# A hybrid pool / mLSTM block on one core: summed weight operands kept in DRAM for the second token half, and another order at the passage to the mLSTM outputs

## The chip, the cores and the metric

One Trainium2 chip; the kernel runs on one of its cores. The metric is the device time of one execution in microseconds (us). It was timed three times before the change: 2134.82, 2144.59 and 2145.74 us, median 2144.59. One more execution was taken by the hardware profiler.

## The reference, cut to what matters

The block takes 2048 tokens of width 1024 and a context of 256 tokens. Both are normalised and modulated, and projected by one matrix `w_in`; the projections feed a pooling mixer and a bidirectional mLSTM whose start state comes from the context. Then follow an output projection, a second norm and a SwiGLU layer. All in float32.

```
hx = modulate(rmsnorm(x, norm1[l]), sh1, sc1)
px, qx, kx, vx, ox, gx = project(hx, w_in[l], ...)     # pool, q, k, v, o, gates
_, st_f, st_b = mlstm_bidir(qc, kc, vc, gc, zero, zero)  # context: states alone
hx_m, _, _ = mlstm_bidir(qx, kx, vx, gx, st_f, st_b)
...
c_new = decay * c0 + einsum('bhs,bhsv,bhsd->bhvd', wk, vc, kc)
h     = num / maximum(abs(den), exp(-m))
...
mix_x = concatenate([pool_x, mlstm_output(hx_m, ox)]) @ w_out[l]
x = x + g1 * mix_x
x = x + g2 * swiglu(modulate(rmsnorm(x, norm2[l])), w_up[l], w_down[l])
```

## The kernel before, in words

**Seven products instead of eight.** A projection onto 2 x 128 output columns is done for one half of the tokens (1024 of 2048) at a time. The weight block of 1024 x 256 is cut into four blocks A11, A12, A21, A22 of 512 x 128, the tokens likewise, and the eight block products are replaced by seven, for which four of the seven weight operands are sums of blocks: s1 = A21 + A22 (operand 3), s2 = s1 - A11 (4), A11 - A21 (5) and A12 - s2 (2). `operands` (L586) makes them: `wsum` (L591) adds on VectorE (L593), `split` (L145) then makes a high part by a cast on ScalarE (L147) and a low part by a subtraction on VectorE (L150). Operands 0 and 1 go to tiles `vt`, the others to `wh` and `wl`, of which there are five buffers each. `unit` (L625) does the seven products, `product` (L614) is one of them: 12 matmuls (L619 to L621). `ORDER` (L263) is the order of the operands, 0, 1, 4, 3, 5, 2, 6.

**The projection stage.** The first token half runs two units for q and k (`conv_unit`, convolution and silu behind them), two for o (`o_unit`, a sigmoid), two for the pooling (`pool_units`), through `run_units` (L670); the second half runs pooling, then q and k. `load_raws` (L658) loads the two weight columns of a unit, 512 KB each, on SP's queue into tiles `raw` (three buffers). The token blocks of a half (`Btile`) are loaded by `load_B` (L551), three of them as they are and four through tiles `hst` with a split. Beside all this run the modulation vectors (`ada_acc`, L525), whose weight rows `adaw` come by SP and are summed on VectorE.

**The last two units with the chunk sums.** The second half's two o units (L896 to L900) are done product by product in turn. Between their products, `chunk_step` (L981) is called: for each of the 2 context and 16 token chunks it loads kT and v (`dma_kv`, L867), transposes kT on TensorE, weights it on VectorE (`delta_a`, L913), multiplies it with v into a PSUM tile `pd` (`delta_b`, L924), and copies the result to the state tiles, the forward half and the backward half each for two pairs of heads: three copies on ScalarE (L938), the one of the backward half's second pair on VectorE (L936). `scan_step` (L940) then adds to state k + 1 the decayed state k, with four vector instructions (L943). The first eight scan steps run inside `chunk_step`, the last seven (L1012) behind the last chunk. `load_wo` (L947) prepares the output matrix in between.

**The mLSTM outputs.** 16 steps, chunk 7 down to 0 and then 15 down to 8 (`order`, L1165). `ml_a` (L1038) loads a chunk's operands, multiplies q and k into the PSUM tile `pqk`, takes eight exponentials on ScalarE (L1064) and multiplies both on VectorE (L1066). `ml_b` (L1069) makes the outputs in the four-bank PSUM tile `po`: L1081 from the chunk itself, L1087 from the two states, which are the forward state of the chunk and the backward one. `prep` (L1106) and `proj` (L1130) do gating, output projection and residual, `second_norm` the second norm. The chunks' work is shifted against each other: `ml_a` one chunk ahead, `prep` one behind `ml_b`, `proj` two.

**What sets the order.** The program is written in the order of the text; a planner then decides for each engine in which order its instructions stand in that engine's queue, from readiness in its own model and the order of the text, and `issue_after` forbids it to put an instruction ahead of a named one on the same engine. Each queue is worked off in order. PSUM has eight banks; a pool that is opened takes the place of closed ones and waits for their last readers. Before the change the output stage's pools lie one behind the other from the first bank: three banks `pm`, four `po`, one `pq`; the last two to be freed, those of `pd`, come under the end of `po` and under `pq`.

## Time and profile before

| what | us |
|---|---|
| timed executions | 2134.82, 2144.59, 2145.74 |
| their median | 2144.59 |
| the profiled execution | 2133.75 |
| its span, first to last instruction | 2132.0 |
| TensorE busy | 2022.3 (95%) |
| VectorE busy | 1411.3 (66%) |
| ScalarE busy | 903.2 (42%) |
| moved by DMA | 397.80 MB, mean 187 GB/s |

The profile shows one execution. PE is TensorE's matmuls, PEld its weight loads, DVE VectorE, ACT ScalarE, POOL GpSimd, SP the queue that issues most DMAs. L619 is line 619 of the kernel. `out<-in` names tiles; where buffers of different tiles share a place, the name is that of one of them (`h` is any token block or state tile). Waits show what an engine was idle for; windows give the busy time of each engine in a stretch, the clock granted to TensorE as a share of full speed, the share of the 16 DMA engines' time and what they moved.

### The profile page before, as it was taken

How to read it: one execution, taken by the hardware profiler on the slowest of the kernel's cores; microseconds unless marked ns; L12 is line 12 of the kernel's file. 1: busy time of each engine (PE TensorE's matmuls, PEld its weight loads, DVE VectorE, ACT ScalarE, POOL GpSimd, SP SyncE). 2: the span in 40 equal slices, each digit the busy share in tenths (PEclk: the TensorE clock that was granted, in tenths of full speed). 3: DMA queues.
4: the chain of work that ended last, by engine and by line, in shares of the span. 5: the costliest groups of instructions: out<-in, count | busy, mean ns of one | idle time of the engine just before them, and what ended most of it. 6: DMA issues, size and time to landing. Idle time of an engine off the chain costs nothing.

```text
span 2132.0 us, 27467 instructions
## 1 busy us (share of the span) xinstructions
PE 2022.3 (95%) x9482; PEld 1641.3 (77%) x9482; DVE 1411.3 (66%) x2398; ACT 903.2 (42%) x1792; POOL 231.5 (11%) x222
## 2 busy tenths in 40 slices
PE   7989999995899998999999999999999999999998
PEld 3988776674687776788888877888888788888887
DVE  6866889877365656766676578776777554447664
ACT  5644644455344544433333344333333344433442
POOL 1000123210333320000000000000000002004121
PEclk9999999996899999999999999999999999999999
DMA  8597666568477775434343267556655584644642
GB/s 278 162 291 230 204 229 197 161 184 231 136 219 238 213 220 176 148 97 147 100 141 112 96 199 249 187 188 203 188 186 194 177 325 141 221 148 157 229 162 99
DMA packets 355059, 397.80 MB, mean 187 GB/s; under 512 B 22388, under 2 KB 243160, under 8 KB 354152
## 3 DMA queue, kind: packets, MB, share of 16 engines
q1 hardware_dynamic: 308976, 324.62, 47.5%
q10 hardware_dynamic: 45944, 71.43, 10.3%
q8 instruction: 74, 1.21, 0.2%
q14 instruction: 65, 0.53, 0.1%
HBM read 269.44 MB, written 126.54 MB: 186 GB/s over the span
## 4 chain that ended last, share of the span: by engine, by line
PE 73%; DMA 11%; DVE 8%; issue 3%; ACT 3%; SPq 1%; POOL 1%; ACTq 0%; DVEq 0%; POOLq 0%
PE pa L619 8%; PE pa L620 8%; PE pa L621 8%; PE pdn L1356 7%; PE pdn L1358 7%; PE pdn L1357 7%; PE pg L619 4%; PE pg L621 4%; PE pg L620 4%; PE pb L619 2%; PE pb L621 2%; PE pb L620 2%; DMA hst<-s_hb 2%; PE pm L1138 2%; PE pm L1140 1%
## 5 line engine op out<-in xcount | busy, mean ns | idle before, releaser
L619 PE MATMUL pa<-h,wh 128*128 128x512 f32 x680 | 271.5, 400 | 8.1 <-ACT p L633 4.6
L621 PE MATMUL pa<-h,wl 128*128 128x512 f32 x680 | 270.6, 399 | 0.0
L620 PE MATMUL pa<-h,wh 128*128 128x512 f32 x680 | 270.4, 398 | 0.0
L147 ACT CAST wh<-ws 128x512 fp32r<-128x512 f32 x224 | 138.3, 620 | 299.1 <-PE pg L620 160.7
L1356 PE MATMUL pdn<-ow,op 128*128 128x512 f32 x616 | 236.8, 389 | 1.0 <-ACT op L147 1.0
L1357 PE MATMUL pdn<-ow,op 128*128 128x512 f32 x616 | 237.5, 389 | 0.0
L1358 PE MATMUL pdn<-ow,op 128*128 128x512 f32 x616 | 237.5, 389 | 0.0
L150 DVE TENSOR_TENSOR op<-ra,op 128x512 fp32r<-128x512 f32 x154 | 121.3, 794 | 156.3 <-ACT op L147 156.1
L150 DVE TENSOR_TENSOR wl<-ws,wh 128x512 fp32r<-128x512 f32 x224 | 156.7, 702 | 56.9 <-ACT wh L147 56.6
L147 ACT CAST op<-ra 128x512 fp32r<-128x512 f32 x154 | 95.2, 621 | 222.5 <-PE pdn L1358 220.0
L620 PE MATMUL pg<-h,wh 128*128 128x512 f32 x448 | 177.9, 397 | 2.4 <-DVE h L150 2.4
L619 PE MATMUL pg<-h,wh 128*128 128x512 f32 x448 | 177.5, 397 | 1.4 <-ACT h L147 1.4
L621 PE MATMUL pg<-h,wl 128*128 128x512 f32 x448 | 177.5, 396 | 1.1 <-DVE wl L150 1.1
L619 PEld LDWEIGHTS pa<-h,wh 128*128 128x128 f32 x680 | 128.9, 190 | 43.4 <-ACT p L633 6.4
L621 PEld LDWEIGHTS pa<-h,wl 128*128 128x128 f32 x680 | 128.9, 190 | 31.0 <-issue 1.2
L620 PEld LDWEIGHTS pa<-h,wh 128*128 128x128 f32 x680 | 128.9, 190 | 29.9 <-issue 0.5
L593 DVE TENSOR_TENSOR ws<-raw 128x512 f32<-128x512 f32 x110 | 78.8, 717 | 99.0 <-DMA raw<-in_w_up_dram 91.7
L1388 POOL TENSOR_TENSOR hr<-hr,o 128x1024 f32<-128x1024 f32 x8 | 21.8, 2740 | 1099.5 <-ACT o L1401 929.8
L1356 PEld LDWEIGHTS pdn<-ow,op 128*128 128x128 f32 x616 | 115.5, 188 | 25.2 <-ACT op L147 1.4
L1358 PEld LDWEIGHTS pdn<-ow,op 128*128 128x128 f32 x616 | 115.6, 188 | 24.2
L1357 PEld LDWEIGHTS pdn<-ow,op 128*128 128x128 f32 x616 | 115.6, 188 | 23.9
L1138 PE MATMUL pm<-h,mh 128*128 128x512 f32 x256 | 107.2, 419 | 7.1 <-ACT mh L147 3.7
(361 smaller groups left out, 4318.6 us busy)
## 6 DMA issues: line engine op xcount, KB each, us to landing
raw<-in_w_up_dram SPq DMA_DIRECT2D x88, 512.0 KB
ra<-s_act SPq DMA_DIRECT2D x66, 512.0 KB
s_act<-adaw SPq DMA_DIRECT2D x84, 256.0 KB
rwt<-s_t SPq DMA_DIRECT2D x77, 256.0 KB
adaw<-in_w_ada_dram SPq DMA_DIRECT2D x64, 256.0 KB
s_act<-g SPq DMA_DIRECT2D x63, 256.0 KB
raw<-in_w_in_dram SPq DMA_DIRECT2D x25, 512.0 KB
s_hb<-hb SPq DMA_DIRECT2D x7, 1792.0 KB
```

The source lines that it names most:

```text
L147: nc.scalar.copy(hi, src)
L150: eng_lo.tensor_tensor(lo, src, r32(hi), op=ALU.subtract)
L593: nc.vector.tensor_tensor(t, a, b, op=op)
L619: nc.tensor.matmul(ps, lhsT=ah[:, k], rhs=B[:, 0, k], start=st, stop=False, **kw)
L620: nc.tensor.matmul(ps, lhsT=ah[:, k], rhs=B[:, 1, k], start=False, stop=False, **kw)
L621: mm_last[0] = nc.tensor.matmul(ps, lhsT=al[:, k], rhs=B[:, 0, k], start=False, stop=(k == 3), **kw)
L1138: nc.tensor.matmul(pt, lhsT=mh[:, k], rhs=w[:, 0, k % 4], start=(k == 0), stop=False)
L1140: nc.tensor.matmul(pt, lhsT=mlo[:, k], rhs=w[:, 0, k % 4], start=False, stop=(k == 7))
L1356: nc.tensor.matmul(ps, lhsT=A[:, 0, ts_], rhs=W[:, 0], start=start, stop=False)
L1357: nc.tensor.matmul(ps, lhsT=A[:, 0, ts_], rhs=W[:, 1], start=False, stop=False)
L1358: nc.tensor.matmul(ps, lhsT=A[:, 1, ts_], rhs=W[:, 0], start=False, stop=stop)
L1388: nc.gpsimd.tensor_tensor(rows[u], rows[u], O[u][:, :, c_], op=ALU.add)
```

## The change

1. A DRAM tensor `s_w` for 6 weight blocks x 4 sums x 2 parts is added. In the first token half `operands` writes the high and low part of each of the four summed operands to it, by SP's queue, after having made them. In the second half it loads these eight tiles instead of making the sums and splits; of the second weight column only the upper half (A22) is then loaded. The weight block's number goes through the units' tuples.
2. In `delta_b` all four copies are done by ScalarE.
3. The last seven scan steps go from behind the last chunk into the loop of the outputs, one behind each of the first seven `ml_b`.
4. The PSUM pools of the output stage: of the three banks `pm`, one lies at the left and two at the right end, so that `po` and `pq` lie on banks that the units and transposes used, and two `pm` banks on those of `pd`. They are used in turn as before.
5. The exponentials of the first `ml_a` wait (in ScalarE's queue) for the last sigmoid alone, and no longer for the last copy of `delta_b`. The gate `copies[-4]` in `prep` now names another copy, since there are more of them.

```diff
     s_g = dram.tile([4, D], F32, name="s_g")
+    s_w = dram.tile([6, 4, 2, P, 512], F32, name="s_w")
...
-    def operands(raws, wp, early=2):
...
+    def operands(raws, wp, early=2, keep_=None, kept=None):
+        SUMS = (4, 3, 5, 2)
+        if kept is not None:
+            def fetch(i):
+                if i in SUMS:
+                    ops = [wp[0].tile([P, 4, P], F32R, name=n, bufs=5) for n in ("wh", "wl")]
+                    for e, t in enumerate(ops):
+                        with tc.issue_after(raw_last[0].ins):
+                            nc.sync.dma_start(r32(t.rearrange("p k c -> p (k c)")), kept[SUMS.index(i), e])
+                    return tuple(ops)
+                src = raws[0][:, 4 * i:4 * i + 4] if i < 2 else raws[1]
+                if i < early:
+                    hi, lo = (vtp.tile([P, 4, P], F32R, name="vt") for _ in range(2))
+                else:
+                    hi = wp[0].tile([P, 4, P], F32R, name="wh", bufs=5)
+                    lo = wp[0].tile([P, 4, P], F32R, name="wl", bufs=5)
+                split(src, hi, lo, nc.scalar, nc.vector)
+                return hi, lo
+            return fetch
...
             split(src, hi, lo, nc.scalar, nc.vector)
+            if keep_ is not None and i in SUMS:
+                for e, t in enumerate((hi, lo)):
+                    nc.sync.dma_start(keep_[SUMS.index(i), e], r32(t.rearrange("p k c -> p (k c)")))
...
-    def load_raws(srcs, other=None):
+    def load_raws(srcs, other=None, kept=False):
...
                 st = rwp.tile([P, KD, P], F32, name="raw")
+            if kept and raws:
+                st, src = st[:, 0:4], src[4 * P:]
...
-        for n, (srcs, sink, after) in enumerate(units):
-            make = operands(load_raws(srcs), [wp])
+        for n, (srcs, sink, after, w, half) in enumerate(units):
+            if half:
+                make = operands(load_raws(srcs, kept=True), [wp], kept=s_w[w])
+            else:
+                make = operands(load_raws(srcs), [wp], keep_=s_w[w])
...
                 nc.sync.dma_start(rows[:, t0:t0 + n], y[:, :n])
-        return in_cols(O_Q + i0 * P), sink, after
+        return in_cols(O_Q + i0 * P), sink, after, i0 // 2, half
...
                 pool_mm(*todo.pop(0))
-        return lambda half: [(in_cols(0), sink_of(0, half), after),
-                             (in_cols(256), sink_of(2, half), flush if half else after)]
+        return lambda half: [(in_cols(0), sink_of(0, half), after, 2, half),
+                             (in_cols(256), sink_of(2, half), flush if half else after, 3, half)]
...
             nc.scalar.dma_start(s_so[i * P:(i + 1) * P, b * 512:(b + 1) * 512], so)
-        return in_cols(O_O + i0 * P), sink, lambda: None
+        return in_cols(O_O + i0 * P), sink, lambda: None, 4 + i0 // 2, half
...
     uns = [o_unit(tmps[u], 1, 2 * u) for u in range(2)]
-    makes = [operands(load_raws(u[0], o), [wp], early=0) for u, o in zip(uns, (None, rxp))]
+    makes = [operands(load_raws(u[0], o, True), [wp], early=0, kept=s_w[u[3]]) for u, o in zip(uns, (None, rxp))]
...
                     o = dsts[d][:, 2 * p_:2 * p_ + 2, :].rearrange("p h v -> p (h v)")
-                    if d and p_:
-                        nc.vector.tensor_copy(o, pd[64:128, 0:258])
-                    else:
-                        copies.append(nc.scalar.copy(o, pd[d * 64:d * 64 + 64, 0:258]))
+                    copies.append(nc.scalar.copy(o, pd[d * 64:d * 64 + 64, 0:258]))
...
         chunk_step()
-    for i in range(NCH // 2, NCH - 1):
-        scan_step(i)
...
     pms = ExitStack()
-    pmp = pms.enter_context(psum("pm", 3))
+    pma = pms.enter_context(psum("pma", 1))
+    pmb = pms.enter_context(tc.tile_pool(name="pmb", bufs=2, space=PSUM, side="right", reuse_waits="tile"))
...
     pqp = p2s.enter_context(psum("pq", 1))
+    n_pm = [0]
+    class Banks:
+        def tile(self, shape, dt, name):
+            n_pm[0] += 1
+            return (pma if n_pm[0] % 3 == 0 else pmb).tile(shape, dt, name=name)
+    pmp = Banks()
...
         nc.gpsimd.tensor_tensor(wb, wb, qd, op=ALU.mult)
-        with tc.issue_after(last_act[0].ins), tc.issue_after(copies[-1 if n == 0 else -1].ins):
+        with tc.issue_after(last_act[0].ins), tc.issue_after((copies[-1] if n else last_act[0]).ins):
...
             H_[t] = ml_b(t, order[t], A_.pop(t))
+        if t < NCH // 2 - 1:
+            scan_step(NCH // 2 + t)
```

## Rows read from the trace of the kernel before

**Rows 1.** Page, part 1: busy us (share of the span) and instructions.
```profile
PE 2022.3 (95%) x9482; PEld 1641.3 (77%) x9482; DVE 1411.3 (66%) x2398; ACT 903.2 (42%) x1792; POOL 231.5 (11%) x222
```

**Rows 2.** Windows by stage: length, busy us per engine (instructions), clock, DMA share, GB/s.
```profile
186.00:318.00 132.00, 124.36 (x516) 96.67 (x515) 113.72 (x196) 77.14 (x124) 16.35 (x43) 0.97 0.68 219
318.00:418.00 100.00, 89.94 (x343) 65.66 (x342) 92.67 (x139) 43.11 (x71) 31.11 (x27) 0.97 0.58 186
418.00:477.00 59.00, 54.96 (x267) 44.71 (x265) 47.20 (x72) 31.85 (x59) 8.35 (x5) 0.97 0.57 176
477.00:517.00 40.00, 24.20 (x104) 19.43 (x104) 28.66 (x58) 17.32 (x43) 2.54 (x2) 0.68 0.78 211
517.00:545.00 28.00, 15.92 (x89) 12.92 (x89) 17.41 (x47) 14.44 (x47) 6.50 (x4) 0.67 0.74 213
545.00:830.00 285.00, 266.92 (x1458) 218.59 (x1456) 156.28 (x310) 123.70 (x378) 88.68 (x69) 0.97 0.65 199
```

**Rows 3.** TensorE's waits, 318 to 418: awaited, us in total, times, longest.
```profile
PE tp L750 <- DVE pd L782: 4.1, 4, 1.6
PE pb L619 <- DVE pre L713: 3.3, 1, 3.3
PE pg L620 <- DVE h L150: 1.2, 1, 1.2
PE tp L750 <- ACT pd L751: 0.8, 1, 0.8
```

**Rows 4.** TensorE's waits, 477 to 545.
```profile
PE pqk L1057 <- DVE raw L1066: 11.1, 3, 6.8
PE pd L930 <- ACT h L938: 6.5, 5, 4.4
PE pb L917 <- DMA kT<-s_k: 5.6, 1, 5.6
...
PE pqk L1057 <- DVE h L936: 1.4, 1, 1.4
```

**Rows 5.** Full stretch (columns as rows 2); SP's stores (ns min/median/max); DMA sizes.
```profile
296.00:326.00 30.00, 30.00 (x116) 22.96 (x117) 26.09 (x39) 13.21 (x23) 10.15 (x7) 0.94 1.01 362
...
L1236 SPq DMA_DIRECT2D s_act<-adaw x84: 319/320/1752, 878.1 to 1672.8; - x84
...
hst<-s_ha ACTq DMA_DIRECT2D x28, 256.0 KB
...
h<-s_hc SPq DMA_DIRECT2D x6, 1024.0 KB
```

**Rows 6.** VectorE's groups, 318 to 418: busy us, mean ns, idle before.
```profile
L150 DVE TENSOR_TENSOR wl<-ws,wh 128x512 fp32r<-128x512 f32 x13 | 9.9, 758 | 0.0
...
L593 DVE TENSOR_TENSOR ws<-ws,raw 128x512 f32<-128x512 f32 x4 | 2.7, 683 | 0.0
```

**Rows 7.** Timelines, 513 to 545, of TensorE, VectorE, ScalarE: start us, us, instructions [idle].
```profile
513.14 3.38 PE L930 MATMUL pd<-vt,kw 128*128 128x129 f32 x12 [0.84 <-ACT h L938]
...
524.02 2.59 PE L1081 MATMUL po<-vt,raw 128*128 128x129 f32 x16
...
540.74 2.76 PE L1081 MATMUL po<-vt,raw 128*128 128x129 f32 x16
...
517.85 1.67 DVE L943 SCALAR_TENSOR_TENSOR h<-h,decx 128x129 f32<-128x129 f32 x6
...
537.59 1.22 DVE L1066 TENSOR_TENSOR raw<-raw,pqk 128x1024 f32<-128x1024 f32 x1 [4.25 <-DMA kT<-s_k]
...
518.24 4.20 ACT L1064 ACTIVATE raw<-raw,tokq 128x128 f32<-128x128 f32 x14
```

**Rows 8.** The copies out of PSUM: VectorE's group, 477 to 517; ScalarE's line.
```profile
L936 DVE COPY h<-pd 64x258 f32<-64x258 f32 x10 | 4.3, 430 | 0.4
...
L938 ACT COPY h<-pd x45: 354/368/372, 437.1 to 516.6; 64x258 f32<-64x258 f32 x45
```

**Rows 9.** TensorE's longest wait, 186 to 318.
```profile
PE pa L619 <- ACT p L633: 3.8, 2, 3.3
```

## The prediction

> **What bounds the kernel now.** I read first the busy times: TensorE is busy for 95% of the 2132.0 us span [rows 1], so a gain can only come from the stretches in which it is not. The second view, busy time by stage, finds them [rows 2]. The reader should compare each length with TensorE's own time: the projection stage's first token half (186 to 318) leaves 132.0 - 124.4 = 7.6 us idle, its second half (318 to 418) 10.1, the last two units with the chunk sums beside them (418 to 477) 4.0. The passage (477 to 545) leaves 15.8 + 12.1 = 27.9 us in 68, at a granted clock of 0.68 and 0.67, a mixture of the two levels 1.2 and 2.4 GHz; the stages around it stand at 0.97. The mLSTM output stage (545 to 830) is 94% busy. The third view says what ended the idle times. In the second half it was VectorE or work queued on it: four waits make 9.4 of the 10.1 us [rows 3], and VectorE is busy 92.7 of those 100 us [rows 2]. In the passage it was a chain: VectorE's product of weights and scores 11.1 us, ScalarE's copy out of PSUM 6.5, one kT transfer 5.6, VectorE's copy 1.4 [rows 4].
>
> **The change part by part.** The sum is made against the profiled execution, 2133.75 us, that is the span of 2132.0 and 1.75 around it. The three timed executions have a median of 2144.59, which is 10.84 above; the profiled one stands at their quick end (2134.82). The sum is a difference, so I add it to the median.
>
> *A, stores in the first half.* Six units each write 8 operands (4 sums, high and low part) of 128 x 512 x 4 bytes = 256 KB: 48 stores, 12.6 MB. Issuing one takes SP 0.32 us, as the equal store of the MLP shows [rows 5], 15 us in 132; behind each on SP wait the weight loads of the next unit, the ada rows and the convolution's outputs. The operand buffer is freed only after its store; there are five of each, a unit uses five, so the next user comes a unit (some 20 us) later. The load on the DMA engines is the real price: 12.6 MB over 132 us is 95 GB/s on top of 219, at a share of 0.68 [rows 2]; in proportion the share becomes 0.68 x 314/219 = 0.97. From 296 to 326, where the token blocks of the second half come in, the engines are already full (1.01 at 362 GB/s [rows 5]). About one unit's stores and the first unit's kept operands fall there: 2.1 + 2.1 - 0.3 (the half weight load that is saved) = 3.9 MB, 10.9 us at 362 GB/s. Bounds: 0, if all of it hides behind the prefetch, and 11. A gain is excluded, since nothing is taken from this half. I take 4: the stalls just behind that stretch were VectorE's [rows 3], not transfers, so the loads have some slack.
>
> By the Trainium skill ("DMA: Bandwidth & Descriptors", the measured table under Bandwidth), transfers should be batched to 1 MiB or more for 75% of peak, with 2.0 us fixed for one; as an estimate a 256 KB store would take 2.6 us, and 48 in a row 125 us of the 132, which would put A near the +26 of R1 below. That rule is about one transfer at a time; the full stretch [rows 5] moved 362 GB/s with 256 KB and 1 MB transfers in flight [rows 5], so the trace doesn't bear it out here.
>
> *B, the second half, four units.* Each loses 4 sums and 4 low parts on VectorE, at 0.683 and 0.758 us [rows 6]: 5.8 us, so 23 of the 92.7 busy us, and four casts on ScalarE. The loads that take their place (2 MB for a unit of some 22 us, beside 186 GB/s at a share of 0.58 [rows 2]) have a whole unit's time to arrive, since the buffers are freed one unit ahead. SP's queue has them behind the raw loads; the ada rows and outputs wait behind them. With a quarter of VectorE's work gone its stalls should mostly go. At most 10.1 us of idle time and 3% of clock, together 13; at least 0, if transfers come late instead. I take -8; what is late next is the pooling chain that stays on VectorE and GpSimd.
>
> *C, the last two units.* Again 11.6 us leave VectorE (47.2 busy of 59 [rows 2]), but here sixteen 256 KB loads stand on SP between the kT and v loads of the chunk steps, and the two units share five buffers, so a kept load that waits for its buffer holds kT behind it. The price of one late kT is 5.6 us [rows 4]. From -4 (all the idle time) to +6; I take -1.
>
> *D, the passage.* Three edits act here. (1) The 28 vector instructions of the last seven scan steps leave the queue between the last chunk and the first output; six take 1.67 us [rows 7], so 7.8 us. (2) The query-key tile no longer lies in a PSUM bank that the chunk sums used, and the first chunk's eight exponentials wait for the last sigmoid only, not for the last copy. They ran in the row of 14 that takes 4.20 us, begun after a table load, 1.7 us after the last chunk's matmuls [rows 7]; now they may run in ScalarE's idle time before (17.3 of 40 busy [rows 2]). (3) The second copy of the backward half goes from VectorE (0.430 us) to ScalarE (0.368) [rows 8]: 17 in all, ten in this stretch, -4.3 us on VectorE and +3.7 on ScalarE; TensorE's next chunk sum and the scan step wait behind it. Now the chain: the last chunk sum ends at 513.14 + 3.38 = 516.5 [rows 7]; two copies (0.7) and one scan step (4 x 0.28 = 1.1) later, at 518.3, the first output's state matmuls may start. Before, they started when the 2.59 us of matmuls from 524.02 ended, at 526.6 [rows 7]: 8 us. The fourth chunk's product waited to 537.59 for operands whose buffer the first output frees [rows 7], so the second output (540.74) and the first projection move with it. Less waiting for VectorE in the chunk steps gives some 2 more: -10. At best the second output follows the first one's drain directly (about 525 for 540.74): -16. At worst the early exponentials, their table load and the fourth copy lengthen the chunk chain on ScalarE (1.3 + 2.4) and nothing is won: +3.
>
> *E, scan steps inside the output stage.* Seven steps get 1.1 us of vector work each. VectorE is busy 156 of 285 us there, so free slots hide it: 0, at most +4 where the output's drain waits. Each step feeds only the next chunk's state matmuls. The gate of the prep loads is now the first copy of the last chunk, one ScalarE copy later: 0.
>
> Sum: 4 - 8 - 1 - 10 + 0 = -15, so 2118.8 for the profiled execution and **2129.6** for the median.
>
> **The rivals.** *R1, the engines fill up (slower).* In place: first half and its handover. The stores need 0.29 of the engines' time, 39 us in 132; if two thirds find no free engine, A is +26, the late second-half operands leave B at 0, kT loads give C +4, D brings -6: +24, 2169. It decides from A = 19, where the other terms are eaten up, and goes past the bound when A and what the others lose make 30. For it: a share of 0.97 and 362 GB/s at the full stretch; against it: what TensorE waited for most in the first half was ScalarE's copy of a product (3.8 us [rows 9]), not a transfer. The skill's rule cited above points to this side.
> *R2, the gain is eaten (no change).* A +6, B -4, C +1, D -5, E +0: -2, 2142.6. For it: the passage also moves 211 to 213 GB/s at shares of 0.78 and 0.74 [rows 2], so a shorter one can meet its transfers.
> *R3, the passage opens fully.* A +2, B -11, C -2, D -16: -27, 2117.6.
> *R4, the change doesn't do what it says.* The order of each engine's queue is set by a planner; it may put the moved scan steps back before the first outputs, since they are ready by then. D is 0, the rest -5: 2139.6.
>
> **How the numbers follow.** Chances: forecast 0.38, R1 0.15, R2 0.25, R3 0.15, R4 0.07. Some 0.5% (10.7 us) is what a measurement of this kernel can tell from no change: the bounds are 2133.9 and 2155.3. The forecast's own spread, from the bounds of its terms, is about 2117 to 2142; three quarters of it lie below 2133.9. Faster: 0.28 + 0.15 + 0.04 from R2 = 0.47; slower: the better part of R1, 0.13; the same: 0.40. The range leaves out 0.1 at either end, most of R1 and the lower half of R3: 2112 to 2152.
>
> **What would show it.** A: the stage of the first half stays at 132 us, its DMA share goes to over 0.9, and no wait for raw, adaw or hst appears in front of VectorE or TensorE that was not there. B: TensorE's waits for VectorE between 318 and 418 fall from 9.4 us to under 3, VectorE's share from 0.93 to 0.7. C: no kT wait over 5.6 us. D: the first output's state matmuls follow the last chunk sum within 3 us, not 10; the fourth product doesn't wait 4 us. E: scan instructions stand between outputs, and TensorE's waits in the output stage don't grow. Wrong would be: a first half that is longer by over 11 us, new waits of the operand tiles on transfers in the second half, or a chunk chain that ends later than 516.5 less what B and C gave.

## The result, and the profile after

The changed kernel's median was 2117.58 us (2114.01 to 2119.32) against 2144.59: a ratio of 0.9887, 95% interval 0.9862 to 0.9912, or -27.0 us where -15 was forecast (2129.6). The profiled executions differ by less: spans of 2132.0 and 2115.9 us, -16.1. A second comparison (e5) gave 2119.6 against 2140.66, 0.9905 (0.9868 to 0.9943), or -21.1. All executions of either kernel in this study together have medians of 2141.1 and 2118.0: the change is worth about 23 us, and one comparison of few executions may be some 4 us off.

Page of after, part 1, as [rows 1]: busy us (share of the span), instructions.

```profile
PE 2015.6 (95%) x9482; PEld 1637.0 (77%) x9482; DVE 1365.8 (65%) x2333; ACT 899.1 (42%) x1787; POOL 227.0 (11%) x222
```

VectorE lost 45.5 us of work and 65 instructions; TensorE's busy time fell by 6.7 us with the same instructions, which fits the higher mean granted clock (0.982, before 0.975). Busy time by stage of after answers to [rows 2] (length, busy us per engine, granted clock, DMA share, GB/s; the stages end some us earlier now):

```profile
183.00:315.00 132.00, 114.87 (x460) 87.56 (x459) 104.12 (x180) 71.85 (x112) 11.07 (x41) 0.95 0.89 289
315.00:415.00 100.00, 97.92 (x395) 73.70 (x394) 77.31 (x118) 41.12 (x67) 32.72 (x27) 1.00 0.87 287
415.00:470.00 55.00, 54.47 (x272) 44.47 (x270) 30.57 (x51) 28.50 (x53) 8.65 (x7) 1.00 0.84 260
470.00:507.00 37.00, 22.18 (x108) 19.16 (x108) 24.88 (x49) 24.98 (x60) 2.79 (x2) 0.72 0.91 232
507.00:530.00 23.00, 13.09 (x62) 9.60 (x61) 19.18 (x46) 12.99 (x43) 5.10 (x3) 0.84 0.86 253
530.00:816.00 286.00, 267.27 (x1480) 219.30 (x1480) 153.16 (x312) 123.34 (x380) 89.31 (x70) 0.98 0.67 199
```

The first half got worse (17 us idle in 132, before 7.6), the second half and the last two units have next to no idle time left and stand at full clock, and the passage is shorter and its clock higher (0.72 and 0.84; before 0.68 and 0.67). TensorE's waits of after say which wait ends last now (awaited, us in total, times, longest): first 183 to 315, as [rows 9], then 315 to 415, as [rows 3], then 470 to 530, as [rows 4].

```profile
PE pb L642 <- DVE pu L794: 6.2, 1, 6.2
PE pa L642 <- ACT p L656: 3.9, 2, 3.0
```

```profile
PE pb L642 <- DVE pre L741: 1.5, 1, 1.5
PE pa L642 <- ACT u L663: 0.5, 1, 0.5
```

```profile
PE pd L958 <- ACT h L963: 7.8, 2, 4.0
PE pqk L1090 <- DVE raw L1099: 6.6, 1, 6.6
PE pd L958 <- ACT h L148: 5.2, 2, 3.7
```

The four rows of 9.4 us in the second half shrank to two of 2.0, and one wait of 6.2 us is new in the first half, behind a pool buffer (pu).

To compare kernels I use six points of each trace, in us from the start of the span. A product's point is the start of its last matmul. Each row is one execution; the median is over the executions of that run.

| kernel | median | first pool matmul | last o product | last chunk sum ends | first output's state matmuls | first projection | span |
|---|---|---|---|---|---|---|---|
| before | 2144.6 | 304.3 | 476.2 | 516.5 | 526.5 | 544.9 | 2132.0 |
| after | 2117.6 | 314.0 | 469.5 | 507.1 | 510.7 | 514.8 | 2115.9 |
| e1 before again | 2143.2 | 301.8 | 474.4 | 515.0 | 526.0 | 544.9 | 2136.1 |
| e2 kept operands alone | 2134.3 | 316.4 | 479.2 | 515.1 | 525.7 | 544.3 | 2144.1 |
| e3 passage alone | 2123.8 | 305.6 | 473.5 | 507.1 | 509.7 | 514.5 | 2121.8 |
| e4 stores alone | 2154.1 | 316.2 | 489.8 | 530.0 | 541.5 | 561.2 | 2146.4 |
| e5 after again | 2119.6 | 313.6 | 470.1 | 506.0 | 512.2 | 514.0 | 2112.2 |
| e6 gate stores on ScalarE | 2127.2 | 309.7 | 468.9 | 501.5 | 506.8 | 511.8 | 2125.4 |
| e7 gate back | 2116.9 | 313.8 | 470.7 | 500.8 | 513.2 | 514.3 | 2113.1 |
| e8 scan steps back | 2121.2 | 314.9 | 470.3 | 509.4 | 512.2 | 516.8 | 2121.1 |
| e9 banks back | 2133.0 | 315.1 | 470.3 | 507.9 | 516.8 | 537.6 | 2133.7 |
| e10 copies back | 2130.7 | 316.1 | 475.1 | 514.8 | 517.6 | 520.7 | 2121.1 |
| e11 two of four kept | 2133.4 | 313.2 | 483.0 | 511.2 | 521.4 | 524.5 | 2130.9 |
| e12 o units alone kept | 2126.3 | 301.9 | 469.5 | 504.9 | 513.0 | 514.8 | 2124.6 |

The kernel before ran beside each group of four: 2139.85 us beside e1 to e4, 2140.66 beside e5 to e8, 2140.09 beside e9 to e12. Differences below are to these, or to e5 where the text says so.

### The profile page after: what moved, and what is told of

Same layout as the page of the kernel before. It is cut to its first block, busy times and chain, and to the rows that moved or that the text cites. A ratio compares the mean times of both kernels' runs of the same rounds, so it can differ in the third digit from the quotient of the medians.

```text
span 2115.9 us, 27589 instructions
## 1 busy us (share of the span) xinstructions
PE 2015.6 (95%) x9482; PEld 1637.0 (77%) x9482; DVE 1365.8 (65%) x2333; ACT 899.1 (42%) x1787; POOL 227.0 (11%) x222
## 4 chain that ended last, share of the span: by engine, by line
PE 74%; DMA 11%; DVE 5%; ACT 4%; issue 3%; SPq 1%; POOL 1%; ACTq 0%; DVEq 0%; POOLq 0%
PE pa L642 8%; PE pa L644 8%; PE pa L643 8%; PE pdn L1392 7%; PE pdn L1393 7%; PE pdn L1394 7%; PE pg L642 4%; PE pg L643 4%; PE pg L644 4%; PE pb L642 2%; PE pb L644 2%; PE pb L643 2%; PE pm L1171 2%; PE pm L1173 2%; PE pm L1172 2%
## 5 line engine op out<-in xcount | busy, mean ns | idle before, releaser
L148 ACT CAST wh<-ws 128x512 fp32r<-128x512 f32 x200 | 123.5, 619 | 281.3 <-PE pg L643 154.2
L151 DVE TENSOR_TENSOR wl<-ws,wh 128x512 fp32r<-128x512 f32 x200 | 136.4, 685 | 55.4 <-ACT wh L148 55.2
L613 DVE TENSOR_TENSOR ws<-raw 128x512 f32<-128x512 f32 x100 | 69.0, 690 | 96.3 <-DMA raw<-in_w_up_dram 92.0
L148 ACT CAST vt<-raw 128x512 fp32r<-128x512 f32 x112 | 69.2, 619 | 96.0 <-PE pb L643 41.2
```

The lines of the kernel that those rows point to most:

```text
L148: nc.scalar.copy(hi, src)
L151: eng_lo.tensor_tensor(lo, src, r32(hi), op=ALU.subtract)
L613: nc.vector.tensor_tensor(t, a, b, op=op)
```

## The experiments

**The kernel before again (e1, no edit).**

> The kernel before, unchanged, for a second profiled execution. In the first comparison the two profiled spans differ by 16.1 us (2132.0 and 2115.9), the two medians by 27.0. Theory 1 (the change is worth 16, and about 11 us of the medians' difference lie in how the kernel before's executions vary, 2134.8 to 2145.7): if this profile takes about 2134, its stages end within 1 us of those of the first; if it takes about 2145, the extra 11 us lie in stages that the change does not touch, and those stages are to be named. Theory 2 (the change itself removes what makes an execution of 2145): the extra 11 us lie between 183 and 545 us of the span, in the products, the passage or the chunk sums.

Measured: 2143.24 us, ratio 1.0014 (0.9997 to 1.0031); the profiled execution took 2137.87. Its first output came at 526.0, within 0.5 us of the first profile, but the stretch from the first to the sixteenth output (start of the state matmuls) took 276.2 us where the first profile had 269.4. So this extra time lies in the output stage, which speaks for theory 1. But the first profiled execution was a quick one, and the changed kernel's was not: beside the 23 us of all executions their difference of 16.1 was too small by some 7 us, and the medians' 27.0 too large by 4, not by 11.

**The operands alone (e2).** The first part of the change without the others:

```diff
+    s_w = dram.tile([6, 4, 2, P, 512], F32, name="s_w")
+            if keep_ is not None and i in SUMS:
+                for e, t in enumerate((hi, lo)):
+                    nc.sync.dma_start(keep_[SUMS.index(i), e], ...)
+            return fetch        # second half: the same tiles loaded
```

> Only the first part of the change: the four summed operands of each of the six q, in and o units are stored in the first token half and loaded in the second; passage, scan steps, PSUM banks and gate as before. Theory 1, by stages: the pool matmuls of the first half start 8 to 11 us later than before (traces of before and after: 304.3 and 314.0), the last o product ends 5 to 7 us earlier (476.1 and 469.5), and what follows keeps that lead, no more: span 4 to 8 us under the first profile of before, 2124 to 2128. Rival (the lead is given back in the passage, since the last chunk sums wait for ScalarE and VectorE anyway): first output at 523 to 525 us as before, span 2130 to 2133. Rival (the passage alone has no worth, all comes from the operands): span 2115 to 2118.

Measured: 2134.34 us, 0.998 (0.9961 to 0.9999), -5.5. The profiled execution was the slowest of its ten (2145.86), so its points before the output stage count, not its span: pool matmuls 12.1 us later than before, the last o product 3.1 later, the first output 0.8 earlier. The second half won back only some 9 us of the 12. The first rival came true in part: what the last products were early or late by hardly moved the first output. The interval ends next to 1, so -5.5 is barely told from nothing.

**The passage alone (e3).**

```diff
-                    if d and p_:
-                        nc.vector.tensor_copy(o, pd[64:128, 0:258])
-                    else:
-                        copies.append(nc.scalar.copy(o, ...))
+                    copies.append(nc.scalar.copy(o, ...))
-    for i in range(NCH // 2, NCH - 1):
-        scan_step(i)
+        if t < NCH // 2 - 1:
+            scan_step(NCH // 2 + t)
-    pmp = pms.enter_context(psum("pm", 3))
+    pma = pms.enter_context(psum("pma", 1))
+    pmb = pms.enter_context(tc.tile_pool(name="pmb", bufs=2, ...))
-        ... tc.issue_after(copies[-1 if n == 0 else -1].ins):
+        ... tc.issue_after((copies[-1] if n else last_act[0]).ins):
```

> Only the other parts: the chunk sums' copies all on ScalarE, the scan steps of the second half inside the loop of the outputs, the PSUM banks of the outputs split one and two, the first exp gated on the last sigmoid; the operands are summed again in the second half as before. Theory 1: last o product at 476 as before; the first output's state matmuls start 7 to 11 us earlier relative to it than before (before: 526.5 - 476.1 = 50.4 us; after: 510.7 - 469.5 = 41.2), of which the output loop gives back 2 to 3: span 5 to 9 us under the first profile of before, 2123 to 2127. Rival (the passage is quick only because VectorE is relieved of the sums before it, so that the parts need each other): 50 us as before, span 2130 to 2134.

Measured: 2123.79 us, 0.9915 (0.9886 to 0.9944), -16.1. From the last o product to the first output's state matmuls it took 36.2 us (before 50.4, after 41.2), more than expected, and with VectorE as loaded ahead of it as before: these parts don't need the others. They carry most of the change.

**The stores alone (e4).** The operands stored in the first half and never read.

```diff
-                make = operands(load_raws(srcs, kept=True), [wp], kept=s_w[w])
+                make = operands(load_raws(srcs), [wp])
```

> Only the stores: the summed operands are stored in the first token half and never read; the second half forms its sums as before. Theory 1 (the stores fill the DMA engines, the small gate stores behind them on the same queue land late, and the pool buffers that take the gate tiles' place are cleared late): pool matmuls of the first half start 8 to 11 us later than before, all that follows is late by the same, span 2139 to 2143. Rival (the late start is made up, since the first half's products run ahead while the pool matmuls are held back): pool matmuls late by as much, but the last o product at 476 to 479, span 2132 to 2136. My forecast had 4 us for this term, between 0 and 11.

Measured: 2154.11 us, 1.0063 (1.0039 to 1.0087), +14.3, beyond either expectation; the first pool matmul came 11.9 us later, the later points of the table 13.4 to 16.3. The wait is the one of after (TensorE's waits, 183 to 317):

```profile
PE pb L625 <- DVE pu L772: 6.7, 1, 6.7
```

So the loads and the saved sums are worth 14.3 + 5.5 = 19.8 us (e2 against e4), and the stores take 14.3 of it back.

**After again (e5, no edit).**

> The changed kernel, unchanged, for a second profiled execution and for more times beside the kernels of this group. Kept operands alone gave -5.5 us (2134.3 against 2139.85), the passage's parts alone -16.1 (2123.8 against 2139.85). Theory 1 (the two add up, since they act at different places): 21 to 22 us under the kernel before. Rival (they need each other, as 27.0 us of the first comparison would say): 25 to 29 us under it.

Measured: 2119.6 us, 0.9905 (0.9868 to 0.9943), -21.1. The two parts' -5.5 and -16.1 add up to -21.6, as theory 1 has it. The interval, -28 to -12 us, holds nearly all of the rival's range too, so only the medians speak for adding up.

**Why the stores cost so much: gate stores on the other queue (e6).** In the trace of after, SyncE's timeline and GpSimd's at the handover from the o units to the pooling (in) units (start us, us, instruction, idle before and what ended it):

```profile
290.01 0.80 SPq L559 DMA_DIRECT2D h<-s_hc  x2
290.91 0.48 SPq L251 DMA_DIRECT2D s_R<-R  x1
...
294.33 0.42 SPq L252 DMA_DIRECT2D s_W<-W  x1
296.96 0.30 SPq L251 DMA_DIRECT2D s_R<-R  x1
299.45 0.30 SPq L252 DMA_DIRECT2D s_W<-W  x1
...
303.03 0.42 SPq L252 DMA_DIRECT2D s_W<-W  x1
```

```profile
304.60 1.20 POOL L773 MEMSET pu<- 128x640 f32 x2 [16.55 <-DMA s_W<-W]
```

The pool buffers take the place of the gate tiles, so they are cleared only after the last of sixteen 8 KB stores, and the product's sum into them waits for that. These stores stand behind two loads of 1 MB here, and their issue stops twice for 2.2 us. In before they were all issued by 293.3, ahead of those loads (294.7), and the buffers were cleared at 294.5.

The queue's order is only half of this. The stores' data came later too, as ScalarE's timelines of before and of after show:

```profile
286.54 0.40 ACT L244 ACTIVATE W<-R,gcols 128x128 f32<-128x128 f32 x1
```

```profile
291.87 0.39 ACT L245 ACTIVATE W<-R,gcols 128x128 f32<-128x128 f32 x1
```

The last store is issued 10.2 us later than in before (303.03 for 292.87). Its data are 5.3 us of that, the two stops 4.4. The first half had fallen behind already: its last o sigmoid starts at 283.5, in before at 278.5.

```diff
-                nc.sync.dma_start(s_W[:, d, h, :], W[o:o + nch])
+                nc.scalar.dma_start(s_W[:, d, h, :], W[o:o + nch])
```

> The changed kernel with the eight s_W stores of the gate chain issued on ScalarE's queue and no longer on SyncE's, which has the operand stores; the eight s_R stores stay. Theory 1 (what costs the first half its 12 us is the late landing of these stores, for which the clearing of the pool buffers waits: TensorE idle from 299.8 to 306.0 in the trace of after): the 6.2 us shrink to 1 to 3, the first pool matmul starts at 308 to 311 (after: 314.0, before: 304.3), and the time is 3 to 6 us under the changed kernel's. Rival (the DMA engines are full, 0.89 of the time in that stage, so the stores land as late from any queue): first pool matmul at 313 to 316, time within 1 us of the changed kernel's. Second rival (ScalarE loses the time of eight issues, 0.3 to 0.4 us each, when it evicts products there): 1 to 3 us slower.

Measured: 2127.16 us, 0.9932 (0.9909 to 0.9956): no better than the changed kernel, by the medians 7.6 us worse, though the intervals overlap. ScalarE's timeline (first two lines) and SyncE's of this kernel:

```profile
290.21 9.08 ACTq L252 DMA_DIRECT2D s_W<-W  x8
299.33 0.58 ACT L663 COPY u<-pa 128x512 f32<-128x512 f32 x1 [9.15 <-DMA s_W<-W]
```

```profile
289.88 9.07 SPq L251 DMA_DIRECT2D s_R<-R  x8
```

Eight stores took 9 us to issue on either queue at once, and ScalarE's copy out of PSUM stood behind them; the 6.2 us wait became one of 5.1 for that copy. So moving half of them to another queue doesn't help; in both kernels the two 1 MB loads were under way, which suggests that these stop the stores, but no run leaves them out. The pool matmuls and the first output came 4 us earlier all the same, and the output stage took that and more back (first to sixteenth output: 283.9 us, after 272.8). Why, the traces don't settle.

**The gate undone (e7).**

```diff
-        with tc.issue_after(last_act[0].ins), tc.issue_after((copies[-1] if n else last_act[0]).ins):
+        with tc.issue_after(last_act[0].ins), tc.issue_after(copies[-1].ins):
```

> The changed kernel with one edit undone: the exps of the first output are again queued behind the last copy of a chunk sum on ScalarE, not behind the last sigmoid only. Theory 1 (the early exps are what brings the first output forward; in the trace of after they take ScalarE from 474.2 to 478.3 and hold the chunk sums up for 4 us, but are then done): the last chunk sum ends 3 to 4 us earlier (at 503 to 504, after: 507.05), the first output's state matmuls start 2 to 5 us later (513 to 516, after: 510.7), span 2 to 5 us longer. Rival (the exps cost the chunk sums as much as they bring): last chunk sum 3 to 4 us earlier and the first output within 1 us of 510.7, span within 1 us. Second rival (the early exps are a loss): first output at 507 to 509, span 2 to 4 us shorter.

Measured: 2116.89 us, 0.9889 (0.9857 to 0.9921): the same as the changed kernel. TensorE's timeline shows why: the chunk sums end 6.2 us earlier (after: 507.05), then the second query-key product waits 7.7 us for VectorE's product of weights and scores, since ScalarE begins the exponentials only at 503.3, behind the last copy.

```profile
499.75 1.06 PE L958 MATMUL pd<-vt,kw 128*128 128x129 f32 x8
508.50 2.04 PE L1090 MATMUL pqk<-h,kT 128*128 128x256 f32 x4 [7.70 <-DVE raw L1099]
513.21 1.16 PE L1120 MATMUL po<-h,wb 64*128 64x129 f32 x16
```

The exponentials take the same ScalarE time ahead of the copies or behind them. The first output moves by 2.5 us, the first projection by 0.5, the time not at all.

**The scan steps undone (e8).**

```diff
+    for i in range(NCH // 2, NCH - 1):
+        scan_step(i)
-        if t < NCH // 2 - 1:
-            scan_step(NCH // 2 + t)
```

> The changed kernel with one edit undone: VectorE's scan steps of the second half stand ahead of the output loop again, not one behind each output. Theory 1 (these steps, 0.6 us an instruction, kept VectorE from the first score product's input in the kernel before): the first output's state matmuls start 3 to 6 us later (514 to 517, after: 510.7) and the output loop gives back 1 to 2 of it: span 2 to 4 us longer. Rival (VectorE has room there, since the passage waits for ScalarE's copies 7.8 us): first output within 1 us of 510.7, span within 1 us.

Measured: 2121.17 us, 0.9909 (0.9882 to 0.9937); the first output 1.5 us later. Beside after's two medians that is 1.6 to 3.6 us, which these intervals don't tell from nothing. The reason is a row of after (VectorE's scan line: count, ns min/median/max, first and last start us):

```profile
L968 DVE SCALAR_TENSOR_TENSOR h<-h,decx x24: 303/345/2434, 507.7 to 524.2; 128x129 f32<-128x129 f32 x24
L968 DVE SCALAR_TENSOR_TENSOR h<-h,decx,h x8: 340/342/1403, 508.8 to 520.0; 128x129 f32<-128x129 f32 x8
```

Written one behind each output, the steps still all ran before the second output (529.9). An instruction takes 0.34 us here, not the 0.6 of the expectation. The planner put the steps where they are ready, in either text: the rival R4, for this edit.

**The banks undone (e9).**

```diff
-    pma = pms.enter_context(psum("pma", 1))
-    pmb = pms.enter_context(tc.tile_pool(name="pmb", bufs=2, ...))
+    pmp = pms.enter_context(psum("pm", 3))
```

> The changed kernel with one edit undone: the outputs' three PSUM banks are one pool again. Undoing the gate moved no time (2116.9 beside 2119.6) and undoing the scan steps' move 1.6 us (2121.2), so of the passage's 16 us some 12 must lie in the banks and in the copies. Theory 1 (the banks carry most of it): the first score product stands behind the last chunk sum again (508 to 512, after: 504.6 against 507.05), the first projection behind the second output (530 to 540, after: 514.8), the granted clock of 470 to 530 us falls from 0.77 to about 0.70, and the time is 6 to 12 us longer. Rival (the copies carry it): first output within 2 us of 510.7, time within 2 us of the changed kernel's.

Measured: 2133.04 us, 0.9956 (0.994 to 0.9972): 13.4 us longer than e5; its interval is clear of after's in the first comparison and meets the end of that in the second. TensorE's timeline of this kernel, and below it that of after:

```profile
505.81 2.06 PE L958 MATMUL pd<-vt,kw 128*128 128x129 f32 x8 [0.42 <-DMA vt<-s_v]
508.75 2.04 PE L1082 MATMUL pqk<-h,kT 128*128 128x256 f32 x4 [0.88 <-ACT h L963]
...
516.76 1.16 PE L1112 MATMUL po<-h,wb 64*128 64x129 f32 x16
...
537.62 0.48 PE L1163 MATMUL pm<-h,mh 128*128 128x512 f32 x1
```

```profile
504.58 1.57 PE L1090 MATMUL pqk<-h,kT 128*128 128x256 f32 x4
505.99 1.05 PE L958 MATMUL pd<-vt,kw 128*128 128x129 f32 x8
...
510.70 1.16 PE L1120 MATMUL po<-h,wb 64*128 64x129 f32 x16
...
514.82 0.51 PE L1171 MATMUL pm<-h,mh 128*128 128x512 f32 x1 [1.69 <-ACT mh L148]
```

With one pool of three the first query-key product waits for the last chunk sum's copy, and the projection's first product stands behind the second output in TensorE's queue. With the split both run among the chunk sums and the first outputs. Four query-key matmuls took 2.04 us there, at a granted clock of 0.50 (508 to 511), the lower of the two levels. In after the first four took 1.57 us; TensorE then worked without a gap from 504 to 507, and the next four took 1.10 us at 1.00 (507 to 511). The windows 470 to 530 of e9 and of after have 0.65 and 0.77:

```profile
470.00:530.00 60.00, 35.17 (x155) 28.35 (x154) 40.86 (x92) 37.05 (x98) 8.05 (x5) 0.65 0.90 237
```

```profile
470.00:530.00 60.00, 35.27 (x169) 28.76 (x169) 44.06 (x94) 37.97 (x102) 7.89 (x5) 0.77 0.89 240
```

What the passage itself loses is small: the second output's state matmuls start 2.7 us later than in after (536.0 for 533.3). Of the 17.8 us between the two spans, 13 arise behind that, in the output stage, and this profile is the slowest of the kernel's nine executions. So the banks' effect on the passage is shown, but not that it makes the 13.4 us.

**The copies undone (e10).**

```diff
-                    copies.append(nc.scalar.copy(o, ...))
+                    if d and p_:
+                        nc.vector.tensor_copy(o, pd[64:128, 0:258])
+                    else:
+                        copies.append(nc.scalar.copy(o, ...))
```

> The changed kernel with one edit undone: one copy in four of the chunk sums is on VectorE again. Theory 1 (VectorE's copies held the chunk sums up, 11 of them from 477 to 516.5 us in the kernel before, 39.4 us, and 478.4 to 507.05 in the changed one): the last chunk sum ends 4 to 7 us later (511 to 514), the first output's state matmuls start 3 to 6 us later, the time is 3 to 6 us longer. Rival (a copy costs the same on either engine, and ScalarE with all of them is the busier one): last chunk sum within 1 us of 507.05 or earlier, time within 2 us of the changed kernel's or shorter.

Measured: 2130.67 us, 0.9947 (0.9928 to 0.9965), 11.1 us longer than e5; with the same standing to after's two intervals, a little deeper in the second. The last chunk sum ends 7.8 us later than in after and the first output's state matmuls start 6.9 later:

```profile
512.90 1.93 PE L958 MATMUL pd<-vt,kw 128*128 128x129 f32 x8
...
517.63 1.16 PE L1123 MATMUL po<-h,wb 64*128 64x129 f32 x16
```

Of the 7.8 us, 2.1 stand already at the first pool matmul, ahead of anything this edit touches, and 5.6 at the last o product: the copies act beside the last two units, more than in the passage. This profile is the quickest of the kernel's seven executions, 6.1 us longer than after's.

Banks and copies undone cost 13.4 and 11.1 us, 24.5 together, where all parts of the passage bring 16.1. That would fit gains which need each other, since the first output waits for the chunk sums and for its own weights. It is not shown: each of these differences has an interval of 6 us or more to either side, and no run undid both.

**Half the bytes (e11).** Two of the four sums kept; the second weight column is then loaded whole again.

```diff
-        SUMS = (4, 3, 5, 2)
+        SUMS = (4, 2)
+                src = ... wsum(A21, A22, ALU.add) if i == 3 else wsum(A11, A21, ALU.subtract)
```

> The changed kernel with two of the four summed operands of a unit kept (those of products 4 and 2, which save two of four sums and two of four splits), so half the bytes stored and loaded; the other two sums are formed again. The stores alone cost 14.3 us, kept operands as a whole gave 5.5. Theory 1 (cost and gain both go with the bytes): first pool matmul at 308 to 310 (before 304.3, after 314.0), last o product within 2 us of 469.5, time within 3 us of the changed kernel's. Rival (the cost arises only where the DMA engines are full, 0.89 of the first half's products, and half the stores fit beside the other traffic): first pool matmul at 304 to 307, last o product at 463 to 467, time 3 to 7 us under the changed kernel's. Second rival (VectorE's share in the second half rises from 0.77 to 0.85 and TensorE's waits for it return): last o product at 472 to 476, time 3 to 6 us longer.

Measured: 2133.44 us, 0.9979 (0.9961 to 0.9996). The first pool matmul came at 313.2, as late as with all four (313.6 to 316.4 in every such kernel but e6), which no theory had: the delay doesn't go with the stores' bytes. In this kernel's SyncE queue the two 1 MB loads stand ahead of the gate stores again, and the pool buffers were cleared at the same time as in after:

```profile
304.59 1.20 POOL L775 MEMSET pu<- 128x640 f32 x2 [15.81 <-DMA s_W<-W]
```

The gain went almost wholly: between the first and the last pool matmul lie 96.4 us (before 95.4, after 84.5). VectorE was busy 79.5 of the 100 us from 315, after's 77.3, yet TensorE waited 6.5 us for pooled data from it. Its busy share isn't what decides; why its order is so much worse here stays open.

**The o units alone (e12).** No stores in the q, k and in units.

```diff
-            if half:
-                make = operands(load_raws(srcs, kept=True), [wp], kept=s_w[w])
-            else:
-                make = operands(load_raws(srcs), [wp], keep_=s_w[w])
+            make = operands(load_raws(srcs), [wp], keep_=s_w[w] if w > 3 and not half else None)
```

> The changed kernel with the operands kept for the two o units alone, whose stores come behind the first half's pool units; the q and in units form their sums again in the second half. Theory 1 (the cost of the stores lies in the q and in units, where the weights of the modulation are streamed too): first pool matmul at 303 to 306 (after: 314.0), the second half's products wait for VectorE again (last pool matmul at 397 to 402, after: 398.5), the last o product ends at 465 to 470, and the time is within 3 us of the changed kernel's, 3 to 6 under that of the passage's parts alone. Rival (the stores of the o units cost the same where they stand): last pool matmul at 403 to 407, last o product at 471 to 475, time 2 to 5 us longer than the changed kernel's.

Measured: 2126.32 us, 0.993 (0.9906 to 0.9955). The expectation misplaced the o units: in the first half their sixteen operand stores are issued from 219.9 to 248.2, ahead of the pooling units. Now the sixteen gate stores stand ahead of the loads (SyncE's timeline), and the pool buffers are cleared 14.6 us earlier than in after (GpSimd's):

```profile
281.39 0.38 SPq L251 DMA_DIRECT2D s_R<-R  x1
...
288.42 0.42 SPq L252 DMA_DIRECT2D s_W<-W  x1
...
290.89 0.98 SPq L559 DMA_DIRECT2D h<-s_hc  x2
```

```profile
290.04 1.20 POOL L770 MEMSET pu<- 128x640 f32 x2 [10.62 <-DMA adacc<-in_b_ada_dram]
```

The first half is as expected, with the pool matmuls even 2.4 us earlier than before. Its DMA engines are no less busy than those of e11, where the delay was whole (windows of e11, then of e12: TensorE does 374 and 407 matmuls, in before 408 at a share of 0.68):

```profile
183.00:285.00 102.00, 91.38 (x374) 70.54 (x373) 85.06 (x149) 59.89 (x92) 5.82 (x9) 0.97 0.78 252
```

```profile
183.00:285.00 102.00, 94.96 (x407) 74.39 (x406) 88.06 (x157) 64.13 (x101) 17.04 (x35) 1.00 0.78 253
```

So a full DMA share doesn't explain the delay, nor do the bytes in proportion. What differs is which units store: 24 stores of the q, k, in and o units in e11, 16 of the o units in e12. The second half gives the lead back, its sums being on VectorE again, so the last o product comes no earlier than in after (469.5 in both), and the time is no shorter than with the passage alone (2123.8): the kept operands of the o units (term C) by themselves bring nothing that can be measured, and theory 1's time was wrong.

## Why the prediction was right or wrong

The direction was right and the time lay in the range, 12 us under the forecast. As a difference it was -27.0 and -21.1, where -15 was forecast. It was not the forecast's own sum that came true:

- *Adding the profile's sum to the median.* The step "the sum is a difference, so I add it to the median" gave no room for the profiled execution being a quick one, though its distance of 10.84 us was on view. The sum of -15 came close to the two profiles' -16.1 and fell some 8 short of the 23 that all executions show.
- *A, +4 between 0 and 11: measured +14.3 (e4; 8 to 19).* The step that failed is pricing the stores by bytes. The share was foreseen well enough (0.97, measured 0.89), but half the bytes delay the pool matmuls as much (e11), and without stores in the q, k and in units the delay is gone at the same share (e12). One part of the mechanism is seen: the small gate stores, which clear the way for the pool buffers, are late themselves and come behind two 1 MB loads in SyncE's queue. The prediction named raw, ada and convolution traffic behind the stores on SP, not these. Of the 9.7 us in after by which the pool matmuls start later, 3.9 are this one wait's growth (6.2, the same place in before 2.3). Some 5 stood already at the last o sigmoid, scattered over waits of about 1 us; why the stores of the q, k and in units cause them stays open. The prediction's estimate by the Trainium skill ("DMA: Bandwidth & Descriptors", Bandwidth), 48 stores of 2.6 us in a row, isn't borne out: this stage moved 289 GB/s, and the stores as a whole cost 14.3 us. The Trainium skill gives the 2.0 us behind it for transfers issued by GpSimd (same page, "Anatomy of one DMA"); these went by SP.
- *B, -8, and C, -1.* Together with the loads that take the sums' place they are worth -19.8 (e2 against e4), more than the bound of -17. By stage, B was read well: from the first to the last pool matmul 10.9 us are saved, TensorE's waits fell to 2.0 us and VectorE's share to 0.77. C's stage (end of the last pool matmul to the last o product) took 71.0 us in after for 76.5, and no kT wait appeared. But those 5.5 us are not C's alone: with the kept operands and the old copies the stage took 78.3 (e2), with the new copies and the old sums 74.1 (e3). The first output hardly sees any of it: with the kept operands it starts at 510.7, without at 509.7 (e3). That +4 for A with -9 for B and C came near the -5.5 of e2 is luck: two errors that cancel.
- *D, -10, between -16 and +3: measured -16.1 with E (e3; -24 to -12).* The rival R3 had -16 for it. Described rightly is the bank of edit 2: the product no longer waits for a bank of the chunk sums (e9). Mis-sized were the other two. The copies, costed at 0.43 against 0.368 us each, were worth 11 us where the banks are split (e10), and the trace places more of that beside the last two units than in the passage. The scan steps, costed as 7.8 us of VectorE in the way, were worth 1.6 to 3.6 us, not told from nothing (e8). The gate, part of edit 2, brought nothing (e7). "Within 3 us of the last chunk sum" came out as 3.7 us, for 10; TensorE's longest wait for VectorE's product of weights and scores hardly changed (6.6 us, before 6.8).
- *E, 0.* It was not measured by itself. The reason given doesn't apply: no scan instruction stands between later outputs (e8's row).

R3's time, 2117.6, is the measured one, but its A of +2 is not. R1 had the right stage and the wrong limit: the stores did cost 14, but not because the engines were full (e11 and e12), and the gains behind them survived. R2's "the gain is eaten" holds for the kept operands: their 20 us are mostly eaten by the 14 of the stores.

What stays open: whether the kept operands, which don't bring the first output forward, shorten the time at all. The medians say 5 to 6 us, with the new passage (2118.0 and 2123.8) as without it (2134.3 and 2139.85). But the intervals of e3 and after overlap, their quickest executions lie 0.9 us apart (2114.9 and 2114.0), and e12 gains nothing. The difference between e3 and after lies in the output stage in the profiles (from the second output's first matmul to the last projection's 290.9 us in e3, 285.8 and 283.8 in after and e5), where two executions of the kernel before differ by as much (288.2 and 294.4). No version beat the changed kernel by more than the noise.

## What to carry to other kernels

Don't price a new transfer by its bytes alone: here half the stores delayed the next units as much as all of them, and a third of them, in other units and at the same DMA share, not at all. Read also what stands behind it: a small store that frees a buffer for another engine makes that engine wait when it lands late. A stretch where TensorE idles at the lower clock can be used by letting the next stage's first products run inside it, here by giving them PSUM banks of their own. Undo such edits one by one and also together: single differences need not add up. If the profiled execution stands at the edge of the runs, forecast from several executions, not from that one's sum.

## What the runs showed of the hardware

Small stores issued after two 1 MB loads held up their issuing engine on two queues at once: eight 8 KB stores took 9.07 us to issue on SyncE and 9.08 on ScalarE (e6), where sixteen took 7.5 us ahead of the loads (before, 285.8 to 293.3), at 0.42 us each. And one unchanged program took from 2133.3 to 2148.4 us: in its two profiles the first output came within 0.5 us, while the stretch from the first to the sixteenth output took 269.4 and 276.2 us, with the same instructions and a granted clock of 0.95 from 530 to 830 in both.
